# Per-layer gate of a hybrid decoder layer: sixteen plain column tiles in place of six plain tiles and five seven-product pairs

## The chip, the cores and the metric

One core of one Trainium2 chip runs the whole layer in one launch. The metric is the device time of that launch in microseconds. The engines are named as the profile names them: PE is TensorE (PEld its weight loads), DVE is VectorE, ACT is ScalarE, POOL is GpSimd, and SP issues most of the DMAs.

## The reference, cut to what matters

The sequence has 512 tokens, the model width is 2048, the MLP width 8192, all in float32, and there is one layer. The change concerns the end of the layer:

```python
f = square(relu(rms_norm(h, norm_mlp_pre) @ mlp_w1)) @ mlp_w2   # 2048 -> 8192 -> 2048
h = h + rms_norm(f, norm_mlp_post)                              # second residual
h = h + sigmoid(h @ ple_gate) * (p @ ple_proj)                  # gate: 2048 x 2048; p has 256 columns
```

Here `rms_norm(f, g) = f * rsqrt(mean(f*f) + 1e-6) * g`.

## The kernel before

Everything is kept transposed: 128 of the 2048 channels on the partitions, the 512 tokens along the free axis, so the residual is 16 rows of 128x512, two to a tile `self.y[i]`. A float32 product is made of three fp32r matmuls (`mm3`, lines 162 to 165): every operand is split into a high part (ACT copies it, L155) and a low part (DVE subtracts, L156); then high times high, high times low, low times high are added up in PSUM. The split of an activation row is called a unit here (`ug[k]`: 128 x 2 x 512).

The work is a list of **strips**. A strip is 512 columns of one weight tile: four blocks of 128, each with one unit and three matmuls, so twelve matmuls. `go` walks through the list: at strip j it first splits the weights of strip j+4 (`shi`, `slo`, five buffers each), takes up to two finished tiles from a waiting list to their evictions, and calls the matmuls of strip j. Everything else hangs on `at(j, fn)`, in quarters of a strip. The order of every engine's instructions is thus written out by these numbers; each engine runs its own in order.

The end of the program, from strip `last` on (`back`, L1571 ff.), goes so:

- Three strips (`add_ple`) compute the rest of `p @ ple_proj`, whose results go to DRAM (`pp_d`).
- `rms_a` sums the squares of f over the channels by matmuls with a column of ones (L487), takes the root, and `rms_b` spreads the factor R over the partitions by four matmuls with the identity (L505). ACT copies R from PSUM to SBUF (`rbf`, L508).
- For each of 16 rows k: `h2_a` multiplies y by R (even rows on DVE, odd rows on POOL, L1588), `h2_b` adds the residual from `h1_d` (L1592) and lets ACT make the high part (L1594), `h2_c` makes the low part (L1597). Each finished pair of rows is stored to `h2_d` in DRAM.
- Six output tiles of the gate are computed plainly (`add_plain`), four and then two together. In a group of four the first 512 input channels are done for all four tiles at once, unit by unit: 48 matmuls for units 0 to 3, and then one strip per tile.
- The other ten tiles go in five pairs (`pair_a`): two tiles at a time by seven products of half size instead of eight (matmuls with 256 moving columns, fourteen strips a pair). For that, sums and differences of weights (`sums`, L316 to L324) and of activation halves (`prep_a`, `prep_g`) are formed, the latter over the rows of y themselves, which are overwritten; the results are put together in `z_evict`.
- `plain_g` and `g_sink` take the sigmoid, multiply by `pp` and add the residual, both loaded from DRAM (`load_ph`). `plain_g` does the two steps on POOL.

Of the kernel before, what the change touches and what calls it, by code (L numbers as in the profile page):

```python
# [34 lines left out]
NTAB = 1039  # L35
H = S // 2
# [2 lines left out]
RMT = 11.5  # L39
WO = (-12, -11, -10, -9, -7, -5)  # L40
NPL = 6
NPG = 6
G6 = (-7, -6)
G4 = 21
LT = (0, 1, 2, 2.75, 3, 4.5, 5, 5.5, 6, 6, 6.75, 8, 8.5, 9.5, 10.5)
# [18 lines left out]
GS = ()  # L64
SG = -2
SH = 0.25
GD = 5
GP = (7,)
GH = 6
GL = 11  # L70
# [3 lines left out]
RO0 = 1.75  # L74
RO1 = 0.5
HO = 2.75
RF0 = 1.75
RF1 = 0.5
SF = 0.7
PMG = (13.5, 15, 18, 20)  # L80
PLE1 = 5
# [54 lines left out]
class Build:  # L136
# [379 lines left out]
    def run(self):  # L516
        tc, nc, A = self.tc, self.nc, self.A
        cp = self.cp = self.pool("const")
        self.wp = self.pool("w")
        self.vec = cp.tile([P, V_N], F32, name="vec")  # L520
        self.ident = cp.tile([P, P], F32, name="ident")
        self.ones = cp.tile([P, 1], F32, name="ones")
        nc.vector.memset(self.ones, 1.0)
        self.scrap = cp.tile([P, 1], F32, name="scrap")
        self.msum = cp.tile([P, S], F32, name="msum")
        self.ps = self.pool("ps", space=bass.MemoryType.PSUM)
        self.rings = {}
        dp = self.pool("dram", space=bass.MemoryType.DRAM)
        for nm, shape in (("bv_d", [NH, NTAB]), ("z_d", [16, P, S]), ("y1_d", [KT, P, S]), ("h1_d", [KT, P, S]), ("h2_d", [KT, P, S]),
                          ("f_d", [DFF // P, P, S]), ("pp_d", [KT, P, S])):  # L530
            setattr(self, nm, dp.tile(shape, F32, name=nm))
        self.vv_d = dp.tile([NB, P, 8, P], F32, name="vv_d")
        with tc.high_priority(offset=PRIO), tc.manual_schedule():
            self.front()
            self.mid()
            self.back()
            self.go()
            assert not self.cur
            for nm in ("fbctx", "zctx", "snctx", "yctx", "cyctx", "cxctx"):
                self.T[nm].close()  # L540
# [847 lines left out]
    def back(self):  # L1388
# [129 lines left out]
        def out_b(c, m, ps):  # L1518
            y = self.y_row(m)
            if c == 0:  # L1520
                act.activation(y, ps, AF.Copy)
            else:
                v.tensor_tensor(y, ps, y, op=ALU.add)
            if c == NCHUNK - 1:
                sq = self.msum if m == 0 else self.sum_tile("fsq")[:, :S]
                act.activation(sq, y, AF.Square)  # L1526
                if m >= KT - 2:
                    sq_last.append(sq)
                elif m:
                    g.tensor_tensor(self.msum, self.msum, sq, op=ALU.add)  # L1530

        def add_full(c, m):
            q, st = {}, []
# [40 lines left out]
        self.add_ple(range(PLE1, 8), "j")  # L1574
        bg = len(self.strips)

        def load_h(k, n):
            if n == 4:
                t = fb_tile("hy").rearrange("p a b n -> p (a b) n")
            else:  # L1580
                t = self.z_tile("hz")
            nc.sync.dma_start(t, self.h1_d[k:k + n].rearrange("a p n -> p a n"))
            for i in range(n):
                T["h"][k + i] = t[:, i, :]

        def h2_a(k):
            y = xs(k)
            (g if k % 2 else v).tensor_tensor(y, y, T["Rf"], op=ALU.mult)  # L1588

        def h2_b(k):  # L1590
            y = xs(k)
            v.scalar_tensor_tensor(y, y, V[:, V_MLPPOST + k:V_MLPPOST + k + 1], T["h"][k], op0=ALU.mult, op1=ALU.add)  # L1592
            ug.append(self.unit((P, 2, S)))
            act.activation(ug[k][:, 0], y, AF.Copy)  # L1594

        def h2_c(k):
            v.tensor_tensor(ug[k][:, 1], xs(k), f32(ug[k][:, 0]), op=ALU.subtract)  # L1597
            if k % 2:
                self.store(self.h2_d[k - 1:k + 1].rearrange("a p n -> p a n"), self.y[k // 2])

        def fb_tile(name):
            return T["fb"].tile([P, 2, 2, S], F32, tag="fy", name=name, bufs=1)

        def load_ph(m):
            if m == 2:
                t = T["ph", m] = self.z_tile("pz"), self.z_tile("pz")
            else:
                t = fb_tile("pz")
                t = T["ph", m] = t[:, 0], t[:, 1]
            for x, src in zip(t, (self.pp_d, self.h2_d)):  # L1610
                nc.sync.dma_start(x, src[m:m + 2].rearrange("a p n -> p a n"))

        def plain_g(i, ps, st, m0=0):
            i += m0
            pp, h = T["ph", i - i % 2]
            o = pp[:, i % 2]
            t = T["fb"].tile([P, S], F32, tag="t2", name="og", bufs=1)
            act.activation(t, ps, AF.Sigmoid)
            g.tensor_tensor(o, o, t, op=ALU.mult)  # L1619
            g.tensor_tensor(o, o, h[:, i % 2], op=ALU.add)  # L1620
            if i % 2:
                self.store(self.out[:, i - 1:i + 1, :], pp, GD)

        def g_sink(m):
            def f(p, ps, st):
                z = self.z_evict(p, ps, st)
                if m < KT - 2:
                    parts = [(r, slice(0, S)) for r in range(2)] if z is not None else []
                else:
                    parts = self.done({2: 0, 7: 2}.get(p, p))  # L1630
                if not parts:
                    return
                (pp, h), zz = T["ph", m], st["z"]
                for r, c in parts:
                    o = zz[:, r, c]
                    act.activation(o, o, AF.Sigmoid)
                    v.tensor_tensor(o, o, pp[:, r, c], op=ALU.mult)
                    v.tensor_tensor(o, o, h[:, r, c], op=ALU.add)
                if m < KT - 2:
                    self.store(self.out[:, m:m + 2, :], z, 2)  # L1640
                elif p == 4:
                    nc.sync.dma_start(self.out[:, m + 1, :], zz[:, 1])
                elif p in (2, 3, 7):
                    nc.sync.dma_start(self.out[:, m, c], o)
            return f

        at(last - 14, load_h, 0, 4)
        at(last, self.flush)
        at(last, self.sqrt_table)
        at(last + RF0, lambda: self.rms_a([self.msum] + sq_last, D, "f"))  # L1650
        at(last + RF0 + RF1, self.rms_b, "f")
        for k in range(4, 8, 2):
            at(last, load_h, k, 2)
        for k in range(KT):
            for i, fn in enumerate((h2_a, h2_b, h2_c)):
                at(max(last + RF0 + RF1 + 0.25, bg + SF * (k - 3) + SG) + i * SH, fn, k)
        at(bg + 0.25, load_h, 8, 4)
        at(bg + 3, load_h, 12, 2)
        at(bg + 5, load_h, 14, 2)
        self.add_plain(bg, [A["ple_gate"][m] for m in range(4)], ug, plain_g, "Rf", (-12, -11, -10, -7))  # L1660
        if NPG > 4:
            self.add_plain(bg + 16, [A["ple_gate"][m] for m in range(4, NPG)], ug,
                           lambda i, ps, st: plain_g(i, ps, st, 4), "Rf", G6)
            at(bg + G4, load_ph, 4)
        ue = {}
        at(bg + GL, load_ph, 0)
        at(bg + GL + 1, load_ph, 2)
        for m in range(NPG, KT, 2):
            b = len(self.strips)
            self.pair_a(b, A["ple_gate"], m, ue, g_sink(m), last=m == KT - 2, offs=GO if m == NPG else None,  # L1670
                        lo=lambda p, m=m: g if p in GP and m == NPG else None)
            at(b + GH, load_ph, m)
        for p, j in zip(ORDER, GX):
            at(bg + j, self.prep_a, ue, p, True, False, g if p in GS else None)
        for p, j in zip(ORDER[2:4], GG):
            at(bg + j, self.prep_g, p)


def T_close(T, nm):
# [92 lines left out]
```

## Time and profile before

| | us |
|---|---|
| median of 3 runs (2458.16 to 2459.91) | 2459.36 |
| the profiled execution | 2458.5 |
| its span | 2456.7 |
| busy PE, DVE, ACT, POOL | 2342.9, 1544.3, 1076.8, 243.5 |
| matmuls recorded | 13178 |

Between the span and the time of the same execution lie 1.8 us. Where two rows of PE follow each other without a wait, the distance of their starts is what a matmul costs; the durations in its rows overlap. The granted clock is 1.00 where TensorE is at its upper level (2.4 GHz) and 0.50 at the lower (1.2 GHz).

### The profile page before, as it was taken

Reading aid. Unit: us, or ns where it says so; the run is one execution under the profiler, and the core shown is the slowest. Engines: PE = TensorE matmul, PEld = TensorE weight load, DVE = VectorE, ACT = ScalarE, POOL = GpSimd, SP = SyncE. Lnnn points to the kernel's source line nnn. Section 1 sums busy time; section 2 is a strip of 40 time slices with the busy share of each in tenths; the row PEclk is TensorE's granted clock in tenths of the full one; section 3 lists DMA queues with packets and bytes.
Section 4 is the critical chain, followed back from the end, with each engine's and each line's share of the span. In section 5 each row is a group of like instructions: output and inputs, shape, how many; then the busy total and the mean of one; then the engine's idle time right before and its main releaser. Section 6 shows DMA issues by size and latency. Waiting matters only on the chain.

```text
span 2456.7 us, 34978 instructions
## 1 busy us (share of the span) xinstructions
PE 2342.9 (95%) x13178; PEld 2046.3 (83%) x13178; DVE 1544.3 (63%) x2543; ACT 1076.8 (44%) x2008; POOL 243.5 (10%) x238
## 2 busy tenths in 40 slices
PE   7999999989999778999999998999999999997899
PEld 6788888777788658999999997888888888886688
DVE  6364755588746789888888886333333333335898
ACT  5354655478733445444444444333223223223454
POOL 4000000134400440000000000000000000112420
PEclk9999999999999889999999999999999999998999
DMA  5452232422234532343433333434333333233644
GB/s 191 159 180 93 99 108 97 133 89 84 82 129 164 191 103 98 127 138 130 136 131 134 134 135 126 159 116 133 112 112 137 121 103 131 101 112 128 223 142 138
DMA packets 114093, 316.75 MB, mean 129 GB/s; under 512 B 11298, under 2 KB 16674, under 8 KB 113924
## 3 DMA queue, kind: packets, MB, share of 16 engines
q1 hardware_dynamic: 94708, 275.13, 34.0%
q10 hardware_dynamic: 19216, 39.39, 4.2%
q8 instruction: 103, 1.69, 0.3%
q14 instruction: 66, 0.54, 0.1%
HBM read 270.37 MB, written 44.11 MB: 128 GB/s over the span
## 4 chain that ended last, share of the span: by engine, by line
PE 62%; DVE 6%; issue 2%; DMA 1%; ACT 1%; POOL 0%; ACTq 0%; DVEq 0%; SPq 0%; POOLq 0%
PE ps_mm L165 20%; PE ps_mm L163 20%; PE ps_mm L164 20%; DVE slo L156 1%; DVE cx L156 1%; DMA fk<-f_d 1%; DVE y L1592 1%; PE ps_t L487 0%; DVE y L442 0%; POOL pz L1619 0%; ACT shi L155 0%; DVE y L1422 0%; DVE cy L156 0%; DVE y L1588 0%; DMA pz<-pp_d 0%
## 5 line engine op out<-in xcount | busy, mean ns | idle before, releaser
L156 DVE TENSOR_TENSOR slo<-raw,shi 128x512 fp32r<-128x512 f32 x802 | 580.0, 729 | 743.1 <-ACT shi L155 727.4
L155 ACT ACTIVATE shi<-raw 128x512 fp32r<-128x512 f32 x804 | 502.2, 629 | 870.5 <-PE ps_mm L164 748.4
L163 PE MATMUL ps_mm<-cx,shi 128*128 128x512 f32 (+1 forms) x2044 | 707.7, 346 | 25.4 <-ACT shi L155 19.8
L164 PE MATMUL ps_mm<-cx,shi 128*128 128x512 f32 (+1 forms) x2044 | 702.1, 343 | 15.0 <-DVE cx L1428 7.5
L165 PE MATMUL ps_mm<-cx,slo 128*128 128x512 f32 (+1 forms) x2044 | 704.0, 344 | 13.0 <-DVE slo L156 10.7
L165 PE MATMUL ps_mm<-cy,slo 128*128 128x512 f32 (+1 forms) x1604 | 555.0, 346 | 6.4 <-DVE slo L156 6.4
L163 PE MATMUL ps_mm<-cy,shi 128*128 128x512 f32 (+1 forms) x1604 | 555.4, 346 | 3.7 <-ACT shi L155 2.0
L164 PE MATMUL ps_mm<-cy,shi 128*128 128x512 f32 (+1 forms) x1604 | 554.9, 346 | 4.1 <-DVE cy L1428 4.1
L163 PEld LDWEIGHTS ps_mm<-cx,shi 128*128 128x128 f32 x2044 | 393.0, 192 | 70.8 <-ACT shi L155 23.5
L165 PEld LDWEIGHTS ps_mm<-cx,slo 128*128 128x128 f32 x2044 | 392.5, 192 | 62.7 <-DVE slo L156 16.6
L164 PEld LDWEIGHTS ps_mm<-cx,shi 128*128 128x128 f32 x2044 | 393.3, 192 | 57.8 <-DVE cx L1428 8.8
L165 PEld LDWEIGHTS ps_mm<-cy,slo 128*128 128x128 f32 x1604 | 305.8, 191 | 44.6 <-DVE slo L156 8.0
L163 PEld LDWEIGHTS ps_mm<-cy,shi 128*128 128x128 f32 x1604 | 305.9, 191 | 40.8 <-ACT shi L155 2.6
L164 PEld LDWEIGHTS ps_mm<-cy,shi 128*128 128x128 f32 x1604 | 305.9, 191 | 40.5 <-DVE cy L1428 4.8
L155 ACT ACTIVATE shi<-wsum 128x512 fp32r<-128x512 f32 x204 | 126.5, 628 | 163.9 <-PE ps_mm L164 87.8
L156 DVE TENSOR_TENSOR slo<-wsum,shi 128x512 fp32r<-128x512 f32 x204 | 138.7, 687 | 44.8 <-ACT shi L155 44.8
L1530 POOL TENSOR_TENSOR msum<-msum,fsq 128x512 f32<-128x512 f32 x13 | 16.9, 1297 | 1288.7 <-ACT fsq L1526 1288.7
L1257 POOL TENSOR_SCALAR al_P<-al_P,ar_sts 128x512 f32<-128x512 f32 (+3 forms) x128 | 74.2, 601 | 63.8 <-ACT al_ph L1279 29.3
L163 PE MATMUL ps_mm<-y,shi 128*128 128x256 f32 x272 | 76.4, 281 | 1.2 <-ACT shi L155 1.2
L1247 ACT ACTIVATE al_P<-al_P,ar_stm 128x512 f32<-128x512 f32 (+3 forms) x128 | 70.4, 554 | 16.1 <-DVE ar_stm L1242 15.8
L165 PE MATMUL ps_mm<-y,slo 128*128 128x256 f32 x272 | 76.1, 280 | 0.8 <-DVE slo L156 0.8
L164 PE MATMUL ps_mm<-y,shi 128*128 128x256 f32 x272 | 75.9, 279 | 0.0
(356 smaller groups left out, 2336.3 us busy)
## 6 DMA issues: line engine op xcount, KB each, us to landing
raw<-in_mlp_w_dram SPq DMA_DIRECT2D x254, 512.0 KB, 3.7
raw<-in_w_in_dram SPq DMA_DIRECT2D x64, 512.0 KB, 3.5
raw<-in_w_out_dram SPq DMA_DIRECT2D x32, 512.0 KB, 3.5
fk<-f_d SPq DMA_DIRECT2D x32, 512.0 KB, 5.0
raw<-in_ple_gate_dram SPq DMA_DIRECT2D x32, 512.0 KB, 4.8
f_d<-z ACTq DMA_DIRECT2D x29, 512.0 KB, 2.8
y<-in_xT_dram SPq DMA_DIRECT2D x16, 256.0 KB, 6.2
raw<-in_w_v_dram SPq DMA_DIRECT2D x8, 512.0 KB, 4.3
```

The costliest lines, as they stand in the source:

```text
L155: nc.scalar.activation(hi, src, AF.Copy)
L156: (eng or nc.vector).tensor_tensor(lo, src, f32(hi), op=ALU.subtract)
L163: mm(ps, whi, ahi, start=start, stop=False)
L164: mm(ps, whi, alo, start=False, stop=False)
L165: mm(ps, wlo, ahi, start=False, stop=stop)
L1247: act.activation(PP[qt, b], PP[qt, b], AF.Exp, scale=-1.0, bias=st["mn"][:, qt, b:b + 1], accum_out=st["sm"][:, qt, b:b + 1])
L1257: pool.tensor_scalar(PP[qt, b], PP[qt, b], st["sm"][:, qt, b:b + 1], 1.0, op0=ALU.mult, op1=ALU.mult)
L1530: g.tensor_tensor(self.msum, self.msum, sq, op=ALU.add)
L1592: v.scalar_tensor_tensor(y, y, V[:, V_MLPPOST + k:V_MLPPOST + k + 1], T["h"][k], op0=ALU.mult, op1=ALU.add)
```

## The change

All 16 tiles of the gate are plain: the first four in one `add_plain` group, the other twelve one after the other with `add_col` (four strips each). The rows of y are no longer overwritten, so the residual is added from the tile where it lies, and `h2_d`, its eight stores and eight loads go. The steps from R to the units run per pair of rows, all on DVE: one 128x1024 multiplication by R, two additions of the residual, and the low parts later. R is read from PSUM where the matmuls left it. The squares of f are added up by DVE, all but the last, where POOL did it and the last two were left to `rms_a`. `rms_a` starts one strip earlier. The table `GT8` says at which strip after `last` each pair is prepared.

```diff
-RF0 = 1.75
-RF1 = 0.5
+RF0 = 0.75
+RF1 = 0.75
+GT8 = (1.75, 2.5, 3, 3.25, 4.25, 7.5, 9.5, 11.25)
...
+        if name in self.direct:
+            self.T["R"] = self.T["R" + name] = ps2
+            return
...
-                if m >= KT - 2:
+                if m == KT - 1:
                     sq_last.append(sq)
                 elif m:
-                    g.tensor_tensor(self.msum, self.msum, sq, op=ALU.add)
+                    v.tensor_tensor(self.msum, self.msum, sq, op=ALU.add)
...
+        def h2_k(k):
             y = xs(k)
-            v.scalar_tensor_tensor(y, y, V[:, V_MLPPOST + k:V_MLPPOST + k + 1], T["h"][k], op0=ALU.mult, op1=ALU.add)
+            v.scalar_tensor_tensor(y, y, V[:, V_MLPPOST + k:V_MLPPOST + k + 1], T["h"][k // 2][:, k % 2], op0=ALU.mult, op1=ALU.add)
             ug.append(self.unit((P, 2, S)))
             act.activation(ug[k][:, 0], y, AF.Copy)
+        def h2_a(i):
+            y, r = self.y[i], T["Rf"]
+            if i == 0:
+                for a in range(2):
+                    v.tensor_tensor(y[:, a], y[:, a], r, op=ALU.mult)
+                    h2_k(a)
+            else:
+                v.tensor_tensor(y, y, r.unsqueeze(1).to_broadcast([P, 2, S]), op=ALU.mult)
+                h2_k(2 * i)
+                h2_k(2 * i + 1)
+        def h2_lo(k):
             v.tensor_tensor(ug[k][:, 1], xs(k), f32(ug[k][:, 0]), op=ALU.subtract)
-            if k % 2:
-                self.store(self.h2_d[k - 1:k + 1].rearrange("a p n -> p a n"), self.y[k // 2])
...
+        def gate_out(m, ps):
+            o, y = T["pp", m // 2][:, m % 2], xs(m)
             t = T["fb"].tile([P, S], F32, tag="t2", name="og", bufs=1)
+            for c in (slice(0, S),) if m < KT - 1 else (slice(0, H), slice(H, S)):
+                act.activation(t[:, c], ps[:, c], AF.Sigmoid)
+                v.tensor_tensor(o[:, c], o[:, c], t[:, c], op=ALU.mult)
+                v.tensor_tensor(o[:, c], o[:, c], y[:, c], op=ALU.add)
+                if m == KT - 1:
+                    nc.sync.dma_start(self.out[:, m, c], o[:, c])
+            if m == KT - 2:
+                nc.sync.dma_start(self.out[:, m, :], o)
+            elif m % 2 and m < KT - 1:
+                self.store(self.out[:, m - 1:m + 1, :], T["pp", m // 2])
...
+        for i in range(KT // 2):
+            j = last + GT8[i]
+            for o, fn, k in zip((0, 0.5, 0.75), (h2_a, h2_lo, h2_lo), (i, 2 * i, 2 * i + 1)):
+                at(j + o, fn, k)
+        self.add_plain(bg, [A["ple_gate"][m] for m in range(4)], ug, lambda i, ps, st: gate_out(i, ps), "Rf",
+                       (-8.25, -7.25, -6.25, -4.75))
+        for m in range(4, KT):
+            self.add_col(A["ple_gate"][m], ug, lambda ps, m=m: gate_out(m, ps), 8)
+        for i in range(KT // 2):
+            at(bg + (10, 11, 16.5)[i] if i < 3 else bg + 8 * i - 4, load_pp, i)
```

On DVE, from the end of the normalisation chain to the first units, the kernel before has this (`slo` is the low part of a weight strip, `cx` a unit, `hy` and `hz` the loaded residual, the number behind y its tile):

```order
L497 TENSOR_TENSOR rsmf<-rsmf 128x4
L156 TENSOR_TENSOR slo<-raw,shi 128x512
L1588 TENSOR_TENSOR y_15751<-y_15751,rbf 128x512
L1588 TENSOR_TENSOR y_15752<-y_15752,rbf 128x512
L1588 TENSOR_TENSOR y_15753<-y_15753,rbf 128x512
L1592 SCALAR_TENSOR_TENSOR y_15751<-y_15751,vec,hy 128x512 x2
L1592 SCALAR_TENSOR_TENSOR y_15752<-y_15752,vec,hy 128x512 x2
L1592 SCALAR_TENSOR_TENSOR y_15753<-y_15753,vec,hz 128x512 x2
L1597 TENSOR_TENSOR cx<-y_15751,cx 128x512 x2
L1597 TENSOR_TENSOR cx<-y_15752,cx 128x512 x2
```

And the changed kernel at the same place on DVE:

```order
L497 TENSOR_TENSOR rsmf<-rsmf 128x4
L156 TENSOR_TENSOR slo<-raw,shi 128x512
L1605 TENSOR_TENSOR y_15750<-y_15750,ps_t 128x512
L1597 SCALAR_TENSOR_TENSOR y_15750<-y_15750,vec,hy 128x512
L1605 TENSOR_TENSOR y_15750<-y_15750,ps_t 128x512
L1597 SCALAR_TENSOR_TENSOR y_15750<-y_15750,vec,hy 128x512
L156 TENSOR_TENSOR slo<-raw,shi 128x512
L1613 TENSOR_TENSOR cx<-y_15750,cx 128x512 x2
L1608 TENSOR_TENSOR y_15751<-y_15751,ps_t 128x1024
L1597 SCALAR_TENSOR_TENSOR y_15751<-y_15751,vec,hy 128x512 x2
L1613 TENSOR_TENSOR cx<-y_15751,cx 128x512
```

Ahead of the first low part (`cx<-y`) stood nine large DVE instructions after that `slo`, six rows' worth; now five stand there, and POOL's share of the multiplications has moved into this queue.

On SP, the queue of the changed kernel around the same time (`raw` is a weight load of the gate, `pz` a load of `pp_d`):

```order
L246 DMA raw<-in_ple_gate_dram 128x1024 x5
L1385 DMA pp_d<-ppo 128x2x512 x2
L1588 DMA hy<-h_d 128x4x512
L1385 DMA pp_d<-ppo 128x2x512
L1591 DMA hz<-h_d 128x2x512 x2
L246 DMA raw<-in_ple_gate_dram 128x1024 x3
L281 DMA raw<-in_ple_gate_dram 128x1024 x2
L1617 DMA pz<-pp_d 128x2x512 x2
L281 DMA raw<-in_ple_gate_dram 128x1024 x3
L1617 DMA pz<-pp_d 128x2x512
```

The residual loads that wait for a used tile (`hy`, the last two `hz`) and the `pz` loads stand ahead of weight loads; the loads of `h2_d` that followed each `pz` are gone.

## Rows read from the trace of the kernel before

**Rows 1.** The page: the chain that ended last, by engine.
```profile
PE 62%; DVE 6%; issue 2%; DMA 1%; ACT 1%; POOL 0%; ACTq 0%; DVEq 0%; SPq 0%; POOLq 0%
```

**Rows 2.** Windows: stretch, length, busy PE, PEld, DVE, ACT, POOL; clock, DMA, GB/s.
```profile
2247.90:2261.60 13.70, 0.82 (x2) 0.29 (x1) 13.70 (x9) 3.56 (x6) 12.71 (x8) 0.57 0.00 0
2261.60:2340.90 79.30, 72.47 (x288) 57.37 (x289) 65.68 (x77) 34.41 (x61) 27.52 (x17) 0.92 0.63 219
2340.90:2451.00 110.10, 104.21 (x841) 102.44 (x839) 98.24 (x153) 51.65 (x94) 16.14 (x6) 0.98 0.43 145
```

**Rows 3.** Timeline of PE: start, duration, instruction, count, and what ended its wait.
```profile
2234.38 0.39 PE L163 MATMUL ps_mm<-cx,shi 128*128 128x512 f32 x1
...
2239.82 0.28 PE L487 MATMUL ps_t<-ones,msum 128*128 128x1 f32 x2
...
2242.42 0.48 PE L163 MATMUL ps_mm<-cx,shi 128*128 128x512 f32 x1
...
2244.52 1.91 PE L505 MATMUL ps_t<-ident,rsmf 128*128 128x128 f32 x8
...
2372.77 0.28 PE L163 MATMUL ps_mm<-cx,shi 128*128 128x256 f32 x1
...
2375.89 0.28 PE L165 MATMUL ps_mm<-cx,slo 128*128 128x256 f32 x1
...
2450.89 0.28 PE L165 MATMUL ps_mm<-y,slo 128*128 128x256 f32 x1
```

**Rows 4.** Chain that ended last, 2246 to 2262 us: start, duration, what.
```profile
2246.47 0.61 ACT rbf L508
...
2247.10 3.55 DVE y L1588 x3
...
2251.06 10.10 DVE y L1592 x6
2261.16 0.61 DVE cx L1597
...
2261.81 0.79 PE ps_mm L164
```

**Rows 5.** Timeline of DVE at 2286 us, where POOL has nothing to do.
```profile
2286.18 0.68 DVE L1588 TENSOR_TENSOR y<-y,rbf 128x512 f32<-128x512 f32 x1
2286.90 0.75 DVE L1592 SCALAR_TENSOR_TENSOR y<-y,vec,hz 128x512 f32<-128x512 f32 x1
2288.35 0.69 DVE L1597 TENSOR_TENSOR cy<-y,cy 128x512 fp32r<-128x512 f32 x1 [0.70 <-ACT cy L1594]
2288.96 0.69 DVE L156 TENSOR_TENSOR slo<-raw,shi 128x512 fp32r<-128x512 f32 x1
```

**Rows 6.** Groups of instructions of DVE by form, 2234 to 2457 us: a large one.
```profile
L316 DVE TENSOR_TENSOR wsum<-raw 128x1024 f32<-128x1024 f32 x5 | 6.1, 1223 | 1.6 <-DMA raw<-in_ple_gate_dram 1.5
```

**Rows 7.** Timeline of DVE and ACT after the last matmul of the MLP.
```profile
2234.58 0.69 DVE L1523 TENSOR_TENSOR y<-ps_mm,y 128x512 f32<-128x512 f32 x1 [1.54 <-PE ps_mm L165]
...
2235.36 0.63 ACT L1526 ACTIVATE fsq<-y 128x512 f32<-128x512 f32 x1 [3.05 <-DVE y L1523]
```

**Rows 8.** Timeline of PE behind a wait in the plain part.
```profile
2294.33 0.79 PE L163 MATMUL ps_mm<-cx,shi 128*128 128x512 f32 x1 [2.02 <-ACT shi L155]
2294.92 0.63 PE L164 MATMUL ps_mm<-cx,shi 128*128 128x512 f32 x1
...
2297.05 0.63 PE L163 MATMUL ps_mm<-cy,shi 128*128 128x512 f32 x1
```

**Rows 9.** Timeline of the last evictions: ACT, DVE, and SP's last issue.
```profile
2449.17 0.42 ACT L1636 ACTIVATE z<-z 128x256 f32<-128x256 f32 x1 [4.54 <-DVE z L393]
2449.62 0.43 DVE L1637 TENSOR_TENSOR z<-z,pz 128x256 f32<-128x256 f32 x1 [0.48 <-ACT z L1636]
...
2453.94 0.33 SPq L1644 DMA_DIRECT2D out_dram<-z  x1
```

**Rows 10.** DMA issues, 2230 to 2457 us: queue, count, size, median us to landing.
```profile
raw<-in_ple_gate_dram SPq DMA_DIRECT2D x28, 512.0 KB, 5.3
...
out_dram<-pz ACTq DMA_DIRECT2D x3, 512.0 KB, 2.6
```

More of the change, by code (lines that the diff above doesn't have):

```diff
@@ L41 @@
 NPL = 6
-NPG = 6
 G6 = (-7, -6)
@@ L527, in run @@
         self.rings = {}
+        self.direct = ("f",)
         dp = self.pool("dram", space=bass.MemoryType.DRAM)
-        for nm, shape in (("bv_d", [NH, NTAB]), ("z_d", [16, P, S]), ("y1_d", [KT, P, S]), ("h1_d", [KT, P, S]), ("h2_d", [KT, P, S]),
+        for nm, shape in (("bv_d", [NH, NTAB]), ("z_d", [16, P, S]), ("y1_d", [KT, P, S]), ("h1_d", [KT, P, S]),
                           ("f_d", [DFF // P, P, S]), ("pp_d", [KT, P, S])):
@@ L1575, in back, with fb_tile, load_h @@
         bg = len(self.strips)
-        def load_h(k, n):
-            if n == 4:
-                t = fb_tile("hy").rearrange("p a b n -> p (a b) n")
-            else:
[L1581 to L1586, printed above, removed]
+        def fb_tile(name):
+            return T["fb"].tile([P, 2, 2, S], F32, tag="fy", name=name, bufs=1)
+        def load_h(i, n):
+            if n == 2:
+                w = fb_tile("hy")
+                t = [w[:, 0], w[:, 1]]
+                nc.sync.dma_start(w.rearrange("p a b n -> p (a b) n"), self.h1_d[2 * i:2 * i + 4].rearrange("a p n -> p a n"))
+            else:
+                t = [self.z_tile("hz")]
+                nc.sync.dma_start(t[0], self.h1_d[2 * i:2 * i + 2].rearrange("a p n -> p a n"))
+            for a in range(n):
+                T["h"][i + a] = t[a]
@@ L1587, in h2_a @@
+        def h2_k(k):
             y = xs(k)
-            (g if k % 2 else v).tensor_tensor(y, y, T["Rf"], op=ALU.mult)
-        def h2_b(k):
-            y = xs(k)
-            v.scalar_tensor_tensor(y, y, V[:, V_MLPPOST + k:V_MLPPOST + k + 1], T["h"][k], op0=ALU.mult, op1=ALU.add)
+            v.scalar_tensor_tensor(y, y, V[:, V_MLPPOST + k:V_MLPPOST + k + 1], T["h"][k // 2][:, k % 2], op0=ALU.mult, op1=ALU.add)
             ug.append(self.unit((P, 2, S)))
             act.activation(ug[k][:, 0], y, AF.Copy)
-        def h2_c(k):
-            v.tensor_tensor(ug[k][:, 1], xs(k), f32(ug[k][:, 0]), op=ALU.subtract)
-            if k % 2:
-                self.store(self.h2_d[k - 1:k + 1].rearrange("a p n -> p a n"), self.y[k // 2])
@@ L1601, in fb_tile @@
[L1601 to L1616, printed above, removed]
-            t = T["fb"].tile([P, S], F32, tag="t2", name="og", bufs=1)
[L1618 to L1645, printed above, removed]
@@ L1647, in back @@
-        at(last - 14, load_h, 0, 4)
+        def h2_a(i):
[9 more added lines that the diff above has]
+        def h2_lo(k):
+            v.tensor_tensor(ug[k][:, 1], xs(k), f32(ug[k][:, 0]), op=ALU.subtract)
@@ new lines, in load_pp @@
+        def load_pp(i):
+            t = T["pp", i] = self.z_tile("pz")
+            nc.sync.dma_start(t, self.pp_d[2 * i:2 * i + 2].rearrange("a p n -> p a n"))
+        def gate_out(m, ps):
+            o, y = T["pp", m // 2][:, m % 2], xs(m)
+            t = T["fb"].tile([P, S], F32, tag="t2", name="og", bufs=1)
+            for c in (slice(0, S),) if m < KT - 1 else (slice(0, H), slice(H, S)):
[8 more added lines that the diff above has]
+                self.store(self.out[:, m - 1:m + 1, :], T["pp", m // 2])
@@ L1648, in back @@
+        at(last - 14, load_h, 0, 2)
+        at(last - 11, load_h, 2, 1)
+        at(last - 9, load_h, 3, 1)
         at(last, self.flush)
-        at(last, self.sqrt_table)
+        at(last + 0.25, self.sqrt_table)
         at(last + RF0, lambda: self.rms_a([self.msum] + sq_last, D, "f"))
         at(last + RF0 + RF1, self.rms_b, "f")
[L1652 to L1676, printed above, removed]
+        for i in range(KT // 2):
+            j = last + GT8[i]
+            for o, fn, k in zip((0, 0.5, 0.75), (h2_a, h2_lo, h2_lo), (i, 2 * i, 2 * i + 1)):
+                at(j + o, fn, k)
@@ new lines, in back @@
+        at(last + GT8[1] + 0.25, load_h, 4, 2)
+        at(last + GT8[2] + 0.25, load_h, 6, 1)
+        at(last + GT8[3] + 0.25, load_h, 7, 1)
+        self.add_plain(bg, [A["ple_gate"][m] for m in range(4)], ug, lambda i, ps, st: gate_out(i, ps), "Rf",
[4 more added lines that the diff above has]
+            at(bg + (10, 11, 16.5)[i] if i < 3 else bg + 8 * i - 4, load_pp, i)
```

## The prediction

> **What bounds the kernel now.** I read the chain of waits first: 62% of it is TensorE [rows 1], so TensorE's time decides, and what counts is where it waits. All of the change lies behind the last matmul of the MLP, so the next view is TensorE's timeline from there. The first of 36 matmuls of the three projection strips starts at 2234.38, the span ends at 2456.7: 222.3 us are in play. The reader should split them in four and set the matmuls' own cost against each part. One 512-column matmul costs (2239.82 - 2234.38)/24 = 0.2267 us, one 256-column matmul (2375.89 - 2372.77)/26 = 0.120 us [rows 3].
>
> - Entry, to the second gate matmul at 2261.81 (one matmul of the gate is behind it, so up to 2261.6): 27.2 us, of which the projection's 36 matmuls need 8.2.
> - Plain part, 24 strips, 288 matmuls: 79.3 us [rows 2] against 65.3.
> - Pairs, 840 matmuls: 110.1 us [rows 2] against 100.8.
> - Tail from the last matmul (2450.89 + 0.12) to the end: 5.7 us.
>
> So 42 us are neither tail nor these matmuls: some 4 are the norm's own matmuls, the rest waits and a low clock. The window view says who works meanwhile: from 2247.9 to 2261.6 TensorE has 0.82 us, DVE is busy all the time and POOL 12.7 of 13.7 us [rows 2]. The chain there runs through DVE: six residual additions take 10.10 us, 1.68 each [rows 4], where the same instruction with an idle POOL takes 0.75 [rows 5]. DVE is thus the bound of the entry, and it is slowed while POOL works on the same rows.
>
> **The change, part by part.**
>
> *Norm.* `rms_a` comes one strip earlier: 12 matmuls, 2.72 us. Its last square is there: ACT ends it at 2235.36 + 0.63 [rows 7], and the sums would start at 2237.10. Eight instead of twelve sums: they took 2242.42 - 2239.82 = 2.60 us [rows 3], so 1.73, end 2238.83. From there to R in PSUM passed 2246.47 - 2242.42 = 4.05 us (chain on DVE and ACT, six projection matmuls at falling clock, the identity matmuls) [rows 3, 4]; I keep it. R stands at 2242.9. ACT's copy, 0.61, goes. DVE can start at t = 0 = 2242.9, where it started at 2247.10: 4.2 us earlier.
>
> *Units.* Prices without POOL: multiplication to addition 0.72, addition to low part through ACT's high part 1.45 (2288.35 - 2286.90), independent 512-wide instructions 0.61 apart [rows 5]. R from PSUM: the trace has no such multiplication; an addition that reads PSUM takes 0.69 [rows 7], as from SBUF. The 128x1024 one is bounded by 1.22 [rows 6] and twice 0.69; I take 1.25, as the shape is that of the former. In the order shown in the change: two rows are multiplied and added by t = 2.9, ACT's high parts end at 3.5, then comes a weight strip's high part, so DVE's `slo` runs from 4.1 and the first low part starts at 4.75. TensorE gets it 0.65 later (2261.81 - 2261.16, [rows 4]), at t = 5.4, which is 2248.3. The projection ends before that, so its lateness costs nothing. Entry: 13.5 us less.
>
> *After that* the first 48 matmuls use units 0 to 3 at 12 matmuls (2.72 us) each, so DVE has time. Carried on in the same way, the low part of unit 3 is there at t = 14.4 where TensorE wants it at 13.6 (wait 0.8); units 4 to 7, needed 0.68 apart, come at 17.5 to 19.4 (together about 1.0); `slo` of the seventh gate strip stands behind pair 4's five instructions and is ready at 24.7 against 23.0 (1.6). From t = 30 on DVE is ahead. That is 3.4 us of waits, and I add 1 us for a lower clock behind the longest: after a wait of 2.0 us TensorE ran seven matmuls at its lower level, 0.43 us apart ((2297.05 - 2294.92)/5) [rows 8], which cost 7 x 0.2 = 1.4 us.
>
> *Plain instead of pairs.* Ten tiles: 480 matmuls at 0.2267 = 108.8 against 840 at 0.120 = 100.8; this costs 8.0 us. In exchange `sums`, `prep_a`, `prep_g` and `z_evict` go, and with them the waits of both parts, (79.3 - 65.3) + (110.1 - 100.8) = 23.3 us, of which 4.4 come back as above: 10.9 us less net (23.3 - 4.4 - 8.0). DVE has per tile four `slo` and two 512-wide instructions, at most 4.1 us of 10.9, so it cannot bound the later tiles.
> The Trainium skill (TensorE: Matmul & The Clock Gate, section Back-to-back issue gap) gives the spacing as the columns over 2.4 GHz plus 2.5 ns; by it the exchange would cost 480 x 0.2158 - 840 x 0.1092 = 11.9 us, an estimate from that page, and the gain would be 4 us smaller. The rows are slower than the page at both widths, and more so at 256, so here the measured spacings decide.
>
> *Squares on DVE.* Thirteen former POOL additions and one more, 0.69 each, in the last sixteen tiles of the MLP. With four `slo` and one addition, DVE has 3.5 us of the 10.9 of such a tile, and the weights are split four strips ahead; cost nothing. If the cover failed, an addition would delay one `slo` by 0.7, inside four strips.
>
> *DMA.* Eight stores and eight loads of 512 KB less. The weight load of a single tile is asked for eight strips ahead, four before its split (10.9 us), and takes 5.3 [rows 10]; cost nothing. `hy` waits for pair 1's additions (t = 8.6) and pair 4 needs it at 21.
>
> *Tail.* Sigmoid, multiplication and addition on halves: an eviction starts 0.2 after the matmul before it is through (2234.58 against 2234.38, [rows 3, 7]), ACT 0.45, then four DVE instructions of 0.43 to the issue, and 2456.7 - 2453.94 = 2.76 behind it [rows 9]: 5.1 against 5.7.
>
> **Sum.** 13.5 + 10.9 + 0.6 = 25.0 us. Counted forward: 2248.3 + 767 x 0.2267 + 4.4 + 5.1 = 2431.7 for the span, 2433.5 with the 1.8 us around it. The profiled execution is 0.9 under the median, so I forecast 2434 us.
>
> **Rivals.**
>
> *DVE and ACT in turn.* Each low part waits for a high part made from DVE's previous result; the row shows 0.70 of idle DVE before it [rows 5]. In the new order two additions or a `slo` stand between, which speaks against it. If DVE lost 0.70 at each of the first eight units, 5.6 us: 2440.
>
> *The clock.* Four short waits remain in the first 25 us; if each cost the 1.4 us of [rows 8], 5.6 us, less the 1 counted: 2439. Against it: three of them are under 1 us. The Trainium skill (TensorE: Matmul & The Clock Gate, Why this matters for your kernels) advises against idle gaps between bursts, since the clock falls; rows 8 agree that it can.
>
> *Slower than before: SP blocks the weights.* Each `pz` load waits for its tile, which the store two pairs earlier must have left, and the weight loads stand behind it. The store is issued three strips before, lands in 2.6 us [rows 10], so some 5.5 us are spare, and 5.6 more in the weights' lead. From 11 us of lateness on TensorE would wait; with six such pairs the change loses when a store lands over 15 us late (11 and 25/6 = 4.2 us a pair); at 17 us late the time is 2434 + 6 x 6 = 2470. No DMA row is near that.
>
> *Little or no change.* If DVE's additions stayed at 1.68 for a reason other than POOL, the entry would give only the 4.2 us of the norm, the pairs their waits of 9.3 less the 8.0 of their saving, and the plain part and tail nothing: about 2454. The 0.75 of the same instruction beside an idle POOL speaks against it [rows 5].
>
> **How the numbers follow.** Forecast, 2428 to 2438: 0.78. DVE and ACT in turn or the clock, 2438 to 2450, alone or together: 0.17. SP: 0.03. Little or no change: 0.02. The lower bound is the sum without any of the 4.4 us of waits and with 1.22 for the large multiplication, 2429, and a little for a shorter chain to R. Above, both middle rivals together give 2444: range 2428 to 2444. A difference under 0.2% (4.9 us) is what a measurement can't tell from none: faster 0.95, within 0.02, slower 0.03.
>
> **What would show it.** POOL has no instruction after the MLP begins its last tiles; the residual additions last about 0.75; the second gate matmul starts near 2248; matmuls 0.2267 apart from about 2273 to the end; first 256-column eviction only in the last tile; last matmul near 2426. It is wrong if TensorE shows waits for `raw`, if the 1024-wide multiplication takes 2 us, or if the granted clock stays under 0.95 in the gate.

## The result, and the profile of the changed kernel

| | median us | ratio to before, 95% interval |
|---|---|---|
| before (4 runs, 2458.16 to 2461.43) | 2459.64 | |
| changed (4 runs, 2429.77 to 2431.86) | 2431.22 | 0.9883 [0.9866, 0.9900] |

The change takes 28.4 us off; 25.4 were forecast. The profiled execution took 2431.86 us with a span of 2430.1. The lines of its page that answer to [rows 1]:

```profile
PE 2345.1 (97%) x12810; PEld 2032.0 (84%) x12810; DVE 1459.0 (60%) x2449; ACT 1043.2 (43%) x1943; POOL 169.3 (7%) x195
PE 65%; DVE 4%; DMA 1%; issue 1%; ACT 1%; POOL 0%; ACTq 0%; DVEq 0%
```

TensorE is busy about as long as before, and its share of the chain rose from 62% to 65%: what went is time in which it waited. Now the stage in windows (columns as in [rows 2]): entry to the second gate matmul; 44 us in which DVE still prepares the units; the rest of the gate; the tail.

```profile
2235.60:2248.10 12.50, 11.56 (x62) 9.36 (x60) 6.86 (x15) 5.70 (x12) 0.00 (x0) 1.00 0.11 42
2248.10:2292.30 44.20, 42.54 (x182) 33.91 (x183) 39.70 (x56) 20.35 (x34) 0.00 (x0) 1.00 0.55 191
2292.30:2425.10 132.80, 132.80 (x587) 109.66 (x585) 47.98 (x71) 34.89 (x58) 0.00 (x0) 1.00 0.36 129
2425.10:2430.10 5.00, 0.05 (x1) 0.00 (x0) 1.61 (x4) 0.66 (x2) 0.00 (x0) 0.94 0.16 52
```

The POOL column (the fifth busy time) is zero throughout and the clock 1.00 up to the tail; from 2292.3 to the tail TensorE has no idle time at all. TensorE's timeline, where [rows 3, 4] stood before (start, duration, instruction, count, and in brackets the wait and what ended it):

```profile
2235.62 0.39 PE L163 MATMUL ps_mm<-cx,shi 128*128 128x512 f32 x1
...
2238.35 0.28 PE L487 MATMUL ps_t<-ones,msum 128*128 128x1 f32 x2
...
2248.37 0.50 PE L164 MATMUL ps_mm<-cx,shi 128*128 128x512 f32 x1 [1.11 <-DVE cx L1613]
...
2257.38 0.50 PE L164 MATMUL ps_mm<-cx,shi 128*128 128x512 f32 x1 [0.55 <-DVE cx L1613]
...
2266.74 0.50 PE L163 MATMUL ps_mm<-cx,shi 128*128 128x512 f32 x1 [0.64 <-ACT shi L155]
...
2424.76 0.39 PE L165 MATMUL ps_mm<-cy,slo 128*128 128x512 f32 x1
```

From the first projection matmul to the end of the span it is 2430.1 - 2235.62 = 194.5 us, against 222.3 before. And DVE in the entry, in answer to [rows 4, 5]:

```profile
2242.95 0.69 DVE L1605 TENSOR_TENSOR y<-y,ps_t 128x512 f32<-128x512 f32 x1 [0.70 <-PE ps_t L505]
2243.67 0.75 DVE L1597 SCALAR_TENSOR_TENSOR y<-y,vec,hy 128x512 f32<-128x512 f32 x1
2244.34 0.68 DVE L1605 TENSOR_TENSOR y<-y,ps_t 128x512 f32<-128x512 f32 x1
2245.05 0.75 DVE L1597 SCALAR_TENSOR_TENSOR y<-y,vec,hy 128x512 f32<-128x512 f32 x1
2247.02 0.69 DVE L156 TENSOR_TENSOR slo<-raw,shi 128x512 fp32r<-128x512 f32 x1 [1.22 <-ACT shi L155]
2247.63 1.28 DVE L1613 TENSOR_TENSOR cx<-y,cx 128x512 fp32r<-128x512 f32 x2
2248.84 1.21 DVE L1608 TENSOR_TENSOR y<-y,ps_t 128x1024 f32<-128x1024 f32 x1
...
2256.03 0.69 DVE L156 TENSOR_TENSOR slo<-raw,shi 128x512 fp32r<-128x512 f32 x1 [1.22 <-ACT shi L155]
```

The residual addition takes 0.75 where it took 1.68. The tail, in answer to [rows 9]:

```profile
2425.18 0.66 ACT L1623 ACTIVATE og<-ps_mm 128x256 f32<-128x256 f32 x2 [10.22 <-PE ps_mm L165]
...
2426.85 0.42 DVE L1625 TENSOR_TENSOR pz<-pz,y 128x256 f32<-128x256 f32 x1
```

### The profile page after: what moved, and what is told of

It is laid out like the page before. It is cut to its first block, busy times and chain, and to the rows that moved or that the text cites. A ratio compares the mean times of both kernels' runs of the same rounds, so it can differ in the third digit from the quotient of the medians.

```text
span 2430.1 us, 33899 instructions
## 1 busy us (share of the span) xinstructions
PE 2345.1 (97%) x12810; PEld 2032.0 (84%) x12810; DVE 1459.0 (60%) x2449; ACT 1043.2 (43%) x1943; POOL 169.3 (7%) x195
## 4 chain that ended last, share of the span: by engine, by line
PE 65%; DVE 4%; DMA 1%; issue 1%; ACT 1%; POOL 0%; ACTq 0%; DVEq 0%
PE ps_mm L165 22%; PE ps_mm L163 22%; PE ps_mm L164 22%; DMA fk<-f_d 1%; DVE slo L156 1%; DVE cx L156 1%; DVE y L442 0%; PE ps_t L487 0%; DVE y L1426 0%; ACT shi L155 0%; DVE cy L156 0%; DVE y L1597 0%; DMA raw<-in_mlp_w_dram 0%; PE ps_t L505 0%; DVE cx L1613 0%
## 5 line engine op out<-in xcount | busy, mean ns | idle before, releaser
L156 DVE TENSOR_TENSOR slo<-raw,shi 128x512 fp32r<-128x512 f32 x804 | 564.5, 706 | 796.4 <-ACT shi L155 784.8
L163 PEld LDWEIGHTS ps_mm<-cx,shi 128*128 128x128 f32 x2004 | 383.5, 191 | 62.7 <-ACT shi L155 17.6
L164 PEld LDWEIGHTS ps_mm<-cx,shi 128*128 128x128 f32 x2004 | 383.6, 191 | 56.3 <-DVE cx L1432 8.8
L165 PEld LDWEIGHTS ps_mm<-cx,slo 128*128 128x128 f32 x2004 | 383.0, 191 | 54.9 <-DVE slo L156 7.9
L164 PEld LDWEIGHTS ps_mm<-cy,shi 128*128 128x128 f32 x1564 | 298.1, 191 | 43.1 <-DVE cy L1432 4.8
L163 PEld LDWEIGHTS ps_mm<-cy,shi 128*128 128x128 f32 x1564 | 298.2, 191 | 42.8 <-ACT shi L155 2.6
L155 ACT ACTIVATE shi<-wsum 128x512 fp32r<-128x512 f32 x174 | 108.0, 628 | 146.4 <-PE ps_mm L164 81.0
L156 DVE TENSOR_TENSOR slo<-wsum,shi 128x512 fp32r<-128x512 f32 x174 | 118.3, 686 | 41.4 <-ACT shi L155 41.4
L163 PE MATMUL ps_mm<-y,shi 128*128 128x256 f32 x232 | 65.2, 281 | 0.9 <-ACT shi L155 0.9
L165 PE MATMUL ps_mm<-y,slo 128*128 128x256 f32 x232 | 64.9, 280 | 0.8 <-DVE slo L156 0.8
L164 PE MATMUL ps_mm<-y,shi 128*128 128x256 f32 x232 | 64.7, 279 | 0.0
L1246 DVE CUSTOM_DVE_ANT_0 al_P<-ps_s,al_tb 128x512 f32<-128x512 f32 (+3 forms) x128 | 56.1, 483 | 2.6 <-PE ps_s L1239 2.1
```

What stands on the lines that cost most here:

```text
L155: nc.scalar.activation(hi, src, AF.Copy)
L156: (eng or nc.vector).tensor_tensor(lo, src, f32(hi), op=ALU.subtract)
L163: mm(ps, whi, ahi, start=start, stop=False)
L164: mm(ps, whi, alo, start=False, stop=False)
L165: mm(ps, wlo, ahi, start=False, stop=stop)
L1246: v.tensor_tensor_reduce(out=PP[qt, b], in0=X["s", qt][b], in1=X["tb"][:, qt * P:], scale=1.0, scalar=3e38, op0=ALU.add, op1=ALU.min, accu ...
```

## The experiments

The start of the projection differs by up to 7 us between these executions. What the edits change does not cause that: the 1982 matmuls ahead of it take 449.25 us in every one of the eleven traces (2234.38 - 1785.13 in the kernel before, 2235.62 - 1786.37 in the changed one), so the difference arises earlier, where all these kernels do the same work; why was not looked into. So each profile was also read from its own first projection matmul, as above:

| kernel | first projection matmul | second gate matmul, later by | span's end, later by |
|---|---|---|---|
| before | 2234.38 | 27.4 | 222.3 |
| before, second profile | 2234.32 | 26.3 | 223.2 |
| before without POOL | 2231.99 | 19.9 | 206.4 |
| before without POOL, new entry, pairs kept | 2228.39 | 12.7 | 196.6 |
| changed with the old entry | 2235.44 | 25.4 | 209.9 |
| changed | 2235.62 | 12.8 | 194.5 |
| changed, two orders of its low parts | 2232.22, 2229.69 | 11.5, 11.5 | 192.4, 192.6 |

Each pair of figures is read from one execution; the two of the kernel before lie 0.9 us apart at the end.

**POOL out of the kernel before.** All that POOL did from the end of the MLP on goes to DVE; order, pairs and norm stay.

```diff
-            (g if k % 2 else v).tensor_tensor(y, y, T["Rf"], op=ALU.mult)
+            v.tensor_tensor(y, y, T["Rf"], op=ALU.mult)
...
-            g.tensor_tensor(o, o, t, op=ALU.mult)
-            g.tensor_tensor(o, o, h[:, i % 2], op=ALU.add)
+            v.tensor_tensor(o, o, t, op=ALU.mult)
+            v.tensor_tensor(o, o, h[:, i % 2], op=ALU.add)
```

(and likewise the sums of squares, `prep_g` and the two low parts of weights that POOL made)

> The kernel before with all POOL work of the gate stage done by DVE in the same order, pairs kept. Theory A (the entry was slow because DVE and POOL disturb each other): residual additions fall from 1.68 to 0.75 us, the chain to the first low part (six multiplications, six additions) takes about 8 us instead of 13.7, and the plain part loses part of its waits; 2446 to 2453. Rival C (POOL does not disturb DVE; only the order and the pairs matter): DVE has 8 + 8 + 12 instructions more of 0.6 to 0.7 us, about 18 us of work, the entry is at least as late as before; 2460 to 2470.

Measured: 2442.22 us (2440.24 to 2443.46, 4 runs), ratio 0.9927 [0.9912, 0.9942]. DVE in its entry:

```profile
2243.55 3.70 DVE L1588 TENSOR_TENSOR y<-y,rbf 128x512 f32<-128x512 f32 x6 [1.33 <-ACT rbf L508]
2247.17 2.73 DVE L1592 SCALAR_TENSOR_TENSOR y<-y,vec,hy 128x512 f32<-128x512 f32 x4
```

DVE does twice the multiplications, and still the four additions take 2.73 where they took 4 x 1.68: giving work to POOL cost DVE more than the work. The gain is larger than either theory gave. The table says why: the entry is 7.5 us shorter (6.4 by the second profile of before), near the 5.7 that theory A gave for its chain, but the part behind it gains another 8 (10). Part of that can be read in the kernel before, beside POOL's `prep_g`:

```profile
2306.29 6.84 POOL L431 TENSOR_TENSOR y<-y,y 128x512 f32<-128x512 f32 x4
```

```profile
2308.51 6.84 DVE L156 TENSOR_TENSOR cx<-y,cx 128x512 fp32r<-128x512 f32 x4
```

```profile
2317.08 0.50 PE L165 MATMUL ps_mm<-cx,slo 128*128 128x512 f32 x1 [3.39 <-DVE slo L156]
```

With POOL silent the same four low parts take 2.49 together (they start at 2297.74), and TensorE has no wait from 2292 to 2330. What each of POOL's later instructions (`prep_g`, sigmoid products, low parts) cost was not taken apart.

**POOL kept busy beside the changed kernel.** The opposite test: ten multiplications on POOL that nobody waits for.

```diff
+            t = T["fb"].tile([P, S], F32, tag="t2", name="scr", bufs=1)
+            g.tensor_tensor(t[:, :NB], T["rf"], T["rf"], op=ALU.mult)
+            for _ in range(10):
+                g.tensor_tensor(t, self.msum, self.msum, op=ALU.mult)
```

> The changed kernel with eleven GpSimd instructions added, the first a small one that waits for the factor of the norm, then ten 128x512 multiplications that read one row of SBUF and write a scratch tile which nobody reads. They stand in no chain; only DVE's and POOL's durations can react. Theory A (POOL at work slows those DVE instructions that read two rows of SBUF): the residual additions and the low parts beside them go from 0.75 and 0.69 to between 1.3 and 1.7 us, the multiplication that reads R from PSUM stays at 0.69 (128x1024: 1.21); the second gate matmul comes 2 to 4 us later, the time is 2434 to 2445. Rival B (the long additions of the kernel before had to do with their own rows, which POOL was writing): all DVE durations stay, the time is 2430 to 2433.

Measured: one run of 2433.49 us. POOL's row, then DVE's:

```profile
2239.61 13.07 POOL L1637 TENSOR_TENSOR scr<-msum 128x512 f32<-128x512 f32 x10
```

```profile
2240.18 0.69 DVE L1605 TENSOR_TENSOR y<-y,ps_t 128x512 f32<-128x512 f32 x1 [0.70 <-PE ps_t L505]
2240.90 1.42 DVE L1597 SCALAR_TENSOR_TENSOR y<-y,vec,hy 128x512 f32<-128x512 f32 x1
...
2244.98 1.35 DVE L156 TENSOR_TENSOR slo<-raw,shi 128x512 fp32r<-128x512 f32 x1 [1.22 <-ACT shi L155]
2246.26 2.97 DVE L1613 TENSOR_TENSOR cx<-y,cx 128x512 fp32r<-128x512 f32 x2
2249.14 1.21 DVE L1608 TENSOR_TENSOR y<-y,ps_t 128x1024 f32<-128x1024 f32 x1
```

Rows that POOL never touches are slowed: addition 0.75 to 1.42, weight low part 0.69 to 1.35, unit low parts 0.64 to 1.49 each. The multiplication that takes R from PSUM stays at 0.69, and the large one at 1.21. One of the two first additions (2242.95) got through in 0.81. The second gate matmul is 15.0 us behind the first projection matmul, 2.2 later, and the end 198.8. The durations refute rival B; the single time lies half a microsecond above B's range and as much under A's, and decides nothing. The Trainium skill (SBUF — State Buffer, section Who interferes with whom) states just this: a VectorE instruction with two inputs in SBUF contends with a GpSimd instruction that reads SBUF; one with at most one SBUF input does not, outside the modes in which it uses two ports. These rows agree, and give the price: 0.75 to 1.42 with both inputs in SBUF, 0.69 unchanged with one in PSUM.

**The old entry in the changed kernel.** Norm a strip later, R copied, odd rows multiplied on POOL, the old spacing of rows; tiles plain, residual in SBUF.

```diff
-RF0 = 0.75
-RF1 = 0.75
+RF0 = 1.75
+RF1 = 0.5
...
+            (g if k % 2 else v).tensor_tensor(y, y, T["Rf"], op=ALU.mult)
+        for k in range(KT):
+            for i, fn in enumerate((h2_m, h2_k, h2_lo)):
+                at(max(last + RF0 + RF1 + 0.25, bg + SF * (k - 3) + SG) + i * SH, fn, k)
```

> The changed kernel (16 plain tiles) with the entry of the kernel before: norm one strip later, R copied to SBUF, odd rows multiplied on POOL, the steps in the old order row by row. Theory A (the entry is worth about 14 us by itself): second gate matmul 27 us after the first projection matmul instead of 12.7, and a few us of waits behind it: 2444 to 2450. Rival B (what the entry loses is given back, since DVE is then ahead for the plain tiles; the gain comes from the tiles' form): under 2438.

Measured: 2444.93 us (2442.06 to 2447.07, 4 runs), ratio 0.9935 [0.9918, 0.9952]. TensorE's first two gate matmuls:

```profile
2252.51 0.79 PE L163 MATMUL ps_mm<-cx,shi 128*128 128x512 f32 x1 [5.68 <-ACT cx L1599]
2260.81 0.80 PE L164 MATMUL ps_mm<-cx,shi 128*128 128x512 f32 x1 [7.50 <-DVE cx L1613]
```

And the same two in the kernel before:

```profile
2253.52 0.80 PE L163 MATMUL ps_mm<-cx,shi 128*128 128x512 f32 x1 [5.59 <-ACT cx L1594]
2261.81 0.79 PE L164 MATMUL ps_mm<-cx,shi 128*128 128x512 f32 x1 [7.50 <-DVE cx L1597]
```

Both long waits of before are back, and 12.6 of the 15.4 us that the stage loses lie ahead of the second gate matmul. Theory A holds.

**The pairs with the new entry.** Kernel before with the changed kernel's norm, R from PSUM and order of units, without POOL; six plain tiles, five pairs and the residual through `h2_d` stay.

```diff
+            if k % 2:
+                self.store(self.h2_d[k - 1:k + 1].rearrange("a p n -> p a n"), self.y[k // 2])
```

(this against the changed kernel's `h2_lo`; everything from `add_plain` on is that of before, with POOL's work on DVE)

> The kernel before (six plain tiles, five pairs, residual through DRAM) with the entry of the changed kernel and nothing on POOL in the stage. Theory A (entry and POOL are most of the gain; exchanging the pairs is worth 8.0 of matmuls against 9.3 of waits): 2430 to 2437. Rival B (the pairs' preparation and eviction work is the main loss): 2443 or more. Rival D (once the entry is clean and POOL idle the pairs run without waits, so their 8 us count): 2421 to 2427, faster than the changed kernel.

Measured: 2432.53 us (2426.83 to 2435.49, 4 runs), ratio 0.9886 [0.9869, 0.9902]. The totals of TensorE's waits between 2241.2 and 2419.4 in its trace (total us, times, longest):

```profile
PE ps_mm L166 <- DVE slo L157: 4.6, 6, 2.5
PE ps_mm L164 <- ACT shi L156: 2.6, 2, 2.2
PE ps_mm L165 <- DVE cx L1613: 1.8, 3, 1.1
```

and the two longest ones:

```profile
2261.06 0.51 PE L164 MATMUL ps_mm<-cx,shi 128*128 128x512 f32 x1 [2.23 <-ACT shi L156]
...
2321.28 0.38 PE L166 MATMUL ps_mm<-cx,slo 128*128 128x256 f32 x1 [2.53 <-DVE slo L157]
```

Theory A holds: with the pairs still there nearly the whole gain is in. The profile is of the fastest of the four runs. The last matmul starts at 2419.23. From the second gate matmul to its end, 2419.35 - 2241.13 = 178.2 us, the matmuls need 287 x 0.2267 + 100.8 = 165.9, so 12.3 us are lost (9.0 of them in these waits, 1.4 in a stretch at the lower clock behind the longest); the changed kernel, which needs 8.0 more, loses 2.7. The first of the two waits lies behind the stores to `h2_d` (ACT issues them), the second behind the preparation of a pair on DVE.

**R copied to SBUF again.**

```diff
-        self.direct = ("f",)
+        self.direct = ()
```

> The changed kernel with R copied to SBUF by ACT again. Theory A: DVE starts 0.6 us later, each multiplication by R lasts the same as from PSUM (0.69 and 1.21), the time rises by 0.6 to 1, to 2431 to 2433. Rival B (reading PSUM is dearer): the multiplications get shorter by 0.1 or more each and make up for the copy, the time is 2430 to 2431.

Measured: one run of 2431.28. From the end of the sums to DVE's start it is 2242.37 - 2238.84 = 3.5 us in place of 2242.95 - 2240.05 = 2.9; the stage takes 195.1:

```profile
2242.37 0.69 DVE L1605 TENSOR_TENSOR y<-y,rbf 128x512 f32<-128x512 f32 x1 [1.33 <-ACT rbf L511]
...
2248.27 1.22 DVE L1608 TENSOR_TENSOR y<-y,rbf 128x1024 f32<-128x1024 f32 x1
```

The same durations from SBUF: theory A; the direct read is worth the copy, 0.6.

**Why was the clock not down behind the sums?** In the changed kernel the six matmuls behind the sums stand 0.23 to 0.31 apart; before they took (2244.52 - 2242.42)/6 = 0.35 each [rows 3]. First test, 24 sums in place of 16:

```diff
-                if m == KT - 1:
+                if m >= KT - 2:
```

> The changed kernel with the last two squares of f left to the norm's matmuls, as before, so 24 one-column sums in place of 16. Theory A (the clock after the sums depends on how long TensorE does only these): the sums take 2.5 in place of 1.7 us, and the projection matmuls behind them fall to the lower level, 0.28 to 0.43 apart; R stands 1.5 to 2 us later and the second gate matmul too, the time is 2432 to 2434. Rival B (the clock was spared because the sums come a strip earlier, or by chance): the matmuls behind stay 0.23 apart, only the 0.8 is lost, the time is 2431 to 2432.5.

Measured: one run of 2430.83. Behind sums that took 2239.01 - 2236.41 = 2.6 us:

```profile
2239.01 0.48 PE L163 MATMUL ps_mm<-cx,shi 128*128 128x512 f32 x1
2239.32 0.39 PE L164 MATMUL ps_mm<-cx,shi 128*128 128x512 f32 x1
2239.55 0.40 PE L165 MATMUL ps_mm<-cx,slo 128*128 128x512 f32 x1
```

Theory A fails, B holds: 0.9 us for the sums and no fall (stage 195.3; the time is 0.2 under B's range). So the kernel before was profiled once more, unchanged.

> The kernel before, unchanged, profiled a second time. Open is why TensorE fell to its lower level behind the 24 sums in the first profile of it and did not in the kernel without GpSimd (same sums, same place). Theory A (it differs from one execution to the next): the six projection matmuls behind the sums may stand 0.23 apart this time, and the second gate matmul then comes 25 to 26 us after the first projection matmul in place of 27.4. Theory B (it belongs to this kernel): the last four of the six stand 0.28 to 0.43 apart again, 27.4. Time 2456 to 2462 in either case.

Measured: 2459.29 us. Behind the sums, and behind the wait of [rows 8], which is there again:

```profile
2242.36 0.48 PE L163 MATMUL ps_mm<-cx,shi 128*128 128x512 f32 x1
2242.67 0.39 PE L164 MATMUL ps_mm<-cx,shi 128*128 128x512 f32 x1
2242.90 0.40 PE L165 MATMUL ps_mm<-cx,slo 128*128 128x512 f32 x1
...
2292.42 0.50 PE L163 MATMUL ps_mm<-cx,shi 128*128 128x512 f32 x1 [2.06 <-ACT shi L155]
...
2293.48 0.40 PE L163 MATMUL ps_mm<-cx,shi 128*128 128x512 f32 x1
2293.72 0.39 PE L164 MATMUL ps_mm<-cx,shi 128*128 128x512 f32 x1
```

Theory A: in one execution the clock fell at both places, in the other at neither. The second gate matmul comes 26.3 us after the first projection matmul, a little later than A said.

**Low parts earlier.** The changed kernel's first waits are for low parts, so those of pairs 0 and 1 are moved ahead of the next weight strip's low part, and pair 4 is prepared a strip later.

```diff
-GT8 = (1.75, 2.5, 3, 3.25, 4.25, 7.5, 9.5, 11.25)
+GT8 = (1.75, 2.5, 3, 3.25, 5.25, 7.5, 9.5, 11.25)
+GTL = ((0.25, 0.25), (0.5, 0.5)) + ((0.5, 0.75),) * 6
...
-            for o, fn, k in zip((0, 0.5, 0.75), (h2_a, h2_lo, h2_lo), (i, 2 * i, 2 * i + 1)):
+            for o, fn, k in zip((0,) + GTL[i], (h2_a, h2_lo, h2_lo), (i, 2 * i, 2 * i + 1)):
```

> The changed kernel with another order on DVE at the entry: the low parts of pairs 0 and 1 run directly behind their additions, ahead of the weight strips' low parts, and pair 4 comes one strip later. Theory A (DVE's order sets the waits that are left there): the wait for the first low part (1.1 us of idle PE, 1.27 us lost) goes, and those for unit 3 (0.7 lost) and the seventh gate strip (1.1 lost) shrink; 2 to 3 us less, 2428 to 2430. Rival B (DVE has no spare time there, so a wait removed appears at the next unit): same as the changed kernel within 1 us, 2430 to 2432, with the waits at units 4 to 7.

Measured: 2426.68 us (2424.04 to 2428.25, 4 runs), ratio 0.9864 [0.9849, 0.9878]: better than both kernels, and than expected. The waits for the low parts of units 0 and 3 are gone; one for DVE is left, at unit 4:

```profile
2256.09 0.50 PE L165 MATMUL ps_mm<-cx,shi 128*128 128x512 f32 x1 [1.36 <-DVE cx L1614]
```

The stage is 2.1 us shorter. The rest of the 4.5 between the medians is not shown to come from this order: in the two profiles the projection starts 3.4 us earlier, ahead of everything that the order changes. Then also the low parts of units 4 and 5 ahead of pair 3:

```diff
-GTL = ((0.25, 0.25), (0.5, 0.5)) + ((0.5, 0.75),) * 6
+GTL = ((0.25, 0.25), (0.5, 0.5)) + ((0.25, 0.25),) + ((0.5, 0.75),) * 5
```

> The variant with the earlier low parts, and now also those of pair 2 (units 4 and 5) ahead of pair 3's multiplication. Theory A (TensorE waits for a low part only because of what stands ahead of it on DVE): the wait of 1.75 us between starts at unit 4 goes, one of about 1 us comes at unit 6, whose low part now stands behind pair 3's three instructions; 2425 to 2428, within 1 us of the variant without this. Rival B (a unit late at the start costs more later): the waits of the first 50 us add up to more than the 2.2 of that variant and the time is 2428 to 2432.

Measured: 2427.49 us (2424.11 to 2431.49, 4 runs), ratio 0.9874 [0.9857, 0.9890].

```profile
2254.16 0.49 PE L164 MATMUL ps_mm<-cx,shi 128*128 128x512 f32 x1 [0.83 <-ACT cx L1600]
2254.89 0.50 PE L165 MATMUL ps_mm<-cx,shi 128*128 128x512 f32 x1 [0.23 <-DVE cx L1614]
```

The wait has moved two units on, as A said, and is now for a high part first. The stage is the same within 0.2 us. That speaks for DVE and ACT as such being behind there, and not their order; no run has less work for them.

## Why the prediction was right, and where its reasons were not

- **Norm, 4.2 us.** DVE starts 2242.95 - 2235.62 = 7.3 us after the first projection matmul; before it was 12.7, so 5.4 were won. The 1.2 above the forecast are the low clock behind the sums, which the prediction carried over and which did not come. Against the second profile of before, where it did not come either, 2245.88 - 2234.32 = 11.6, the step is worth 4.2. That the second gate matmul starts at 2248.37, where 2248.3 was said, is luck: the projection began 1.2 us later in this execution.
- **Units, t = 5.4.** From DVE's start to the second gate matmul: 2248.37 - 2242.95 = 5.4; the first low part starts at 4.7, where 4.75 was said. The large multiplication takes 1.21 (1.25).
- **Waits, 3.4 and 1.0 for the clock.** From 2248.37 to the end of the last matmul at 2424.99 it is 176.6 us, 767 x 0.2267 is 173.9: 2.7 lost. Unit 3 is late by 0.94 - 0.23 = 0.7 (0.8), units 4 to 7 by 0.3 (1.0), the seventh strip by 1.0 (1.6); there it is ACT's high part, not DVE's low part, that comes last. The clock stayed at 1.00.
- **Plain instead of pairs, 10.9 net.** The size is near: from the second gate matmul to the last matmul's end 189.2 before, 176.6 after, 12.6. The reason given holds only in part. The prediction wrote "In exchange `sums`, `prep_a`, `prep_g` and `z_evict` go, and with them the waits of both parts". With the work of all four kept but POOL silent and the entry new, that stretch takes 178.2: 11.0 of the 12.6 went without the exchange, which itself is worth 1.6, and 0.6 more in the tail. With the pairs 12.3 us are lost in that run, with plain tiles 2.7. So the exchange took 9.6 us of lost time away where 23.3 - 4.4 = 18.9 were forecast, and 8.0 of these are paid back by the plain tiles' dearer matmuls. The old entry agrees: with plain tiles the stretch is 2440.22 - 2260.81 = 179.4, before without POOL, pairs kept, 2432.77 - 2251.89 = 180.9, 1.5 apart. POOL's price was counted where the chain showed it, in the entry, and not in the waits behind. The sum came out all the same because the change ends POOL's work together with the pairs'.
- **Tail, 5.1.** 2430.1 - 2424.99 = 5.1.
- **Costs set at nothing.** TensorE waits nowhere for a weight load, and there is no wait in the last 133 us: the loads stayed hidden. So did the squares on DVE: the 449.25 us ahead of the projection are the same in both kernels.

The four rivals: DVE and ACT do not work in turn at the units (the first low part follows `slo` without a pause), though DVE twice waits 1.22 for the high part of a weight strip, at 2256.03 right ahead of unit 3's low part; the clock did not fall; SP blocked nothing; and the additions did not stay at 1.68. Over the stage 27.8 us went where 25.0 were forecast: 1.2 more in the entry, 1.7 more in the waits.

Taken one after the other, in the table of stages: POOL silent 16 us, the new entry 10 more, the plain tiles 2 more. The shares depend on the order: with the old entry, the plain tiles and the end of POOL's work in them take 12.4 (222.3 to 209.9), and the new entry without POOL then 15.4. And that plain tiles beat the pairs once the entry is new is not shown by the times: the medians are 2431.22 and 2432.53, and the runs with the pairs spread from 2426.83 to 2435.49.

## What to carry to other kernels

Before work is given to GpSimd to relieve VectorE, look for VectorE instructions with two SBUF inputs beside it: if their duration is twice that of the same row elsewhere in the trace, taking the work back can be the gain. A wait belongs to an edit only when a kernel that has the edit alone loses it; half of the lost time that was put down to the pairs (9.3 of 18.9 us) came from elsewhere. Where one profile shows a lower clock, take a second before pricing it.

## What was not expected of the hardware

- The clock behind the same instructions differs between executions of one kernel: behind 24 one-column sums the next matmuls took 0.35 us each in one profile [rows 3] and 0.23 in the next, and behind a wait of 2 us 0.43 [rows 8] and 0.23. Whether the chip they ran on matters was not tested.
- Behind the waits of 1.1 us and less in the changed kernel there was no fall. With the pairs and the new entry it fell behind the wait of 2.53 (256-column matmuls 0.21 apart in place of 0.12 from 2322.04 to 2325.24) and not behind that of 2.23. In the trace with POOL busy TensorE fell to its lower level behind the longest one (granted clock 0.50 from 2249.20 to 2252.00):

```profile
2247.83 0.50 PE L164 MATMUL ps_mm<-cx,shi 128*128 128x512 f32 x1 [3.34 <-DVE cx L1613]
...
2249.51 0.63 PE L164 MATMUL ps_mm<-cx,shi 128*128 128x512 f32 x1
2249.94 0.63 PE L165 MATMUL ps_mm<-cx,slo 128*128 128x512 f32 x1
```
